# One step of a hybrid decoder on one core: LayerNorm's sums at set places between the projection's products, one-part sums of squares, factors spread without diagonals, norm vector loaded first

## The chip, the core and the metric

The kernel runs on one core of a Trainium2 chip. The metric is device time in microseconds (us), as the median of several executions. A profile is a record of one further execution, whose own time is given beside its span.

The engines named below: TensorE (PE, and PEld for its weight loads), VectorE (DVE), ScalarE (ACT), GpSimd (POOL), and SyncE (SP), which issues the transfers. Each works through its own list of instructions in order; semaphores make one wait for another.

## The reference

One layer is computed for 288 tokens (256 of a prompt, 32 of eight samples). What matters here:

```python
def layernorm(x, g, b):
    xf = x.astype(jnp.float32)
    mu = jnp.mean(xf, axis=-1, keepdims=True)
    var = jnp.mean(jnp.square(xf - mu), axis=-1, keepdims=True)
    y = (xf - mu) * lax.rsqrt(var + EPS)
    return (y * g.astype(jnp.float32) + b.astype(jnp.float32)).astype(x.dtype)
...
    h = rmsnorm(x, norm1_g)
    proj = jnp.einsum("btd,de->bte", h, w_in) + b_in
    a, gate, z = proj[..., :D_CONV], proj[..., D_CONV:2 * D_CONV], proj[..., 2 * D_CONV:]
    u = a * jax.nn.sigmoid(gate)
    u_ext = jnp.concatenate([hist_conv.astype(u.dtype), u], axis=1)
    c = jax.nn.silu(layernorm(depthwise_causal_conv(u_ext, conv_w, conv_b), ln_g, ln_b))
    z_ext = jnp.concatenate([hist_pool.astype(z.dtype), z], axis=1)
    d = multiscale_pool(z_ext, pos0)
    p = jnp.einsum("btgc,gce->btge", d, pool_w).reshape(bsz, T, D_POOL) * pool_scale
    mix = jnp.concatenate([c, p], axis=-1)
    x = x + jnp.einsum("btm,md->btd", mix, w_out)
    h2 = rmsnorm(x, norm2_g)
    f = jnp.square(jax.nn.relu(jnp.einsum("btd,df->btf", h2, w_ff1)))
    x = x + jnp.einsum("btf,fd->btd", f, w_ff2)
```

The width is 2048 (1024 of it convolution, 1024 pooling), the hidden width 8192; a last RMSNorm follows. All arrays are float32, and the states of convolution and pooling are outputs too.

## The kernel before

**Layout.** Channels lie on the 128 partitions, the 288 tokens along the free axis. `xT` holds the 16 channel tiles of x; all products give 128 output channels by 288 tokens in one PSUM bank.

**Products.** A float32 operand is split into a high part (a cast to `fp32r`, on ACT) and a low part (the rest, on VectorE or POOL). One term of a product is three matmuls: high weight by high x (L293), high weight by low x (L294), low weight by high x (L295). `gemm` does so for all k and for two banks of output channels; it takes a dictionary `between`, which calls a function ahead of a given k and holds the products from that k on behind the matmul that the function returns. Weights come 128 x 1024 at a time (`load`), are cast (L253, `whi`) and split (L258 on VectorE, L261 on POOL, `wlo`). Five buffers of `whi` and five of `wlo` are there, so a cast can wait until TensorE is done with an older block.

**Stages.** First come the input products: pairs for the eight convolution tiles (c0 to c7 of the list SEQUENCE) and for the four pooling groups, with the pooling matrices' products (L460) between them. The convolution itself is 30 multiply-adds for each tile on VectorE (L411). Then the output projection runs in two halves of eight groups with 48 products each: `project_pool` multiplies the pooling half of w_out with `mixp` and adds to `xT` (L505, the drain of a group), and the loop at L540 multiplies the convolution half with `mixc`, the normalised columns. Then the second norm, the MLP in four chunks, and the last norm with its output multiplications (L617).

**LayerNorm.** POOL adds up the convolution's tiles in `sum_c` (L420). Two matmuls with `ones` sum over the partitions (L512, `pmean`), VectorE subtracts the mean (L515), ACT squares (L517), VectorE adds three of the four squares (L521). `rsqrt_rows` makes 1/sqrt of the sums for each token and spreads it over all partitions. Then each pair of tiles is multiplied with it (L526), put through SiLU with gain and offset (L529), cast (L531) and split (L532).

**The sums of squares.** `rsqrt_sums` takes a list of parts (128 x 288 each). For each third of the tokens (96) it multiplies every part, as stationary operand, with a column of `ones` (L220), so that the tokens' sums come to lie on 96 partitions in three columns. Six small instructions form 1/sqrt (L223 to L230), then three make diagonal matrices from them (L233, `dg`), and `spread` multiplies `ones` with the diagonals (L239), which puts each factor on all partitions. It is used four times: for the first norm (`first_sums`, `first_rows`), LayerNorm, the second norm, and the last one. A float32 matmul of the program shows as two passes in the profile.

**Order.** The program is written in the order of the source, but a scheduler orders each engine's list: it takes what its own estimate of time says is ready, by a priority that follows the source. `later()` lowers the priority of the convolution's taps, and `tc.issue_after(x)` puts the instructions made within it behind x on their engine. `project_pool` before had no such places, so LayerNorm's small matmuls went between its products wherever the scheduler saw them ready. Tiles of a pool with one buffer (`ms`, which holds `pmean` and `pt`) follow each other: the next one waits until the last reader of the one before is through.

## Time and profile before

| what | us |
|---|---|
| median of 3 executions (1105.16 to 1105.8) | 1105.24 |
| the profiled execution's own time | 1111.87 |
| its span | 1110.1 |
| TensorE busy in it | 1089.5 |
| VectorE busy | 640.2 |
| ACT busy | 470.8 |

Busy times of one execution don't add up to the span, since engines work beside each other. Of the 8112 products of 128 x 288, nearly all stand back to back. In a row of the timeline the first two numbers are the start and the length of a group in us; then come the engine, the line, the operation, what it writes and reads with the tile's shape, and in brackets how long the engine had been idle before it and what ended that. Products overlap in the engine's pipeline: one of 0.29 us is followed by the next after about 0.13 us. Rows of windows give the stretch, its length, busy time and count for PE, PEld, DVE, ACT and POOL, then the granted TensorE clock, the share of the DMA engines and GB/s.

### The profile page before, as it was taken

The page shows a single profiled execution, that of the slowest core. Times are in us where ns is not written, and L with a number is a line of the kernel's source. Part 1 is how long each engine was busy: PE and PEld are TensorE (multiplying, and loading weights), DVE is VectorE, ACT ScalarE, POOL GpSimd, SP SyncE. Part 2 cuts the span into 40 slices and gives each one's busy share as a digit, 9 for nine tenths or more (in the row PEclk, how much of TensorE's full clock was granted, in tenths as well). Part 3 has the DMA queues.
Part 4 walks back from the last instruction along what each step waited for, and adds up shares of the span by engine and source line. Part 5 has one row for each costly group of instructions (what it writes and reads, how often), then busy time and mean ns, then how long its engine had stood idle before and what let it go on. Part 6 is the DMA issues. An engine that isn't in the chain of part 4 may idle for free.

```text
span 1110.1 us, 19698 instructions
## 1 busy us (share of the span) xinstructions
PE 1089.5 (98%) x8196; PEld 1086.4 (98%) x8196; DVE 640.2 (58%) x827; ACT 470.8 (42%) x577; POOL 181.5 (16%) x208
## 2 busy tenths in 40 slices
PE   9999999989999999999999999999999999999995
PEld 9999999989999999999999999999999999999995
DVE  7899999578555544445544444455544445554453
ACT  8534554466444433334443333444433334444441
POOL 0889989503000000000000000000000000000000
PEclk9999999999999999999999999999999999999998
DMA  9754467535455555555555555555555555555522
GB/s 328 246 184 147 156 179 230 180 115 171 153 170 169 160 166 170 169 163 164 170 168 162 165 171 167 163 165 171 169 160 166 172 166 163 166 171 164 164 72 86
DMA packets 57113, 187.04 MB, mean 168 GB/s; under 512 B 6080, under 2 KB 11200, under 8 KB 57024
## 3 DMA queue, kind: packets, MB, share of 16 engines
q1 hardware_dynamic: 56608, 185.52, 52.1%
q8 instruction: 64, 1.05, 0.4%
q10 hardware_dynamic: 416, 0.27, 0.1%
q14 instruction: 25, 0.20, 0.0%
HBM read 181.49 MB, written 4.28 MB: 167 GB/s over the span
## 4 chain that ended last, share of the span: by engine, by line
PE 90%; DVE 6%; POOL 2%; issue 1%; ACT 0%; DMA 0%; DVEq 0%; ACTq 0%; POOLq 0%
PE ac L293 30%; PE ac L295 30%; PE ac L294 29%; DVE pc L411 3%; POOL s L440 1%; DVE wlo L258 1%; POOL wlo L261 1%; DVE xT L617 0%; PE pt L220 0%; DMA vec<-in_vec 0%; DVE dx L452 0%; POOL prd L415 0%; DVE dx L464 0%; DVE c L417 0%; PE pt L239 0%
## 5 line engine op out<-in xcount | busy, mean ns | idle before, releaser
L253 ACT CAST whi<-wr 128x1024 fp32r<-128x1024 f32 (+1 forms) x341 | 355.6, 1043 | 569.8 <-PE ac L294 530.5
L258 DVE TENSOR_TENSOR wlo<-wr,whi 128x1024 fp32r<-128x1024 f32 (+1 forms) x300 | 371.9, 1240 | 352.3 <-ACT whi L253 351.5
L293 PE MATMUL ac<-ax,whi 128*128 128x288 f32 x1024 | 303.4, 296 | 0.0
L293 PE MATMUL ac<-fx,whi 128*128 128x288 f32 x1024 | 303.1, 296 | 0.0
L295 PE MATMUL ac<-ax,wlo 128*128 128x288 f32 x1024 | 301.9, 295 | 0.0
L295 PE MATMUL ac<-fx,wlo 128*128 128x288 f32 x1024 | 301.9, 295 | 0.0
L294 PE MATMUL ac<-ax,whi 128*128 128x288 f32 x1024 | 298.5, 292 | 0.0
L294 PE MATMUL ac<-fx,whi 128*128 128x288 f32 x1024 | 298.5, 292 | 0.0
L294 PEld LDWEIGHTS ac<-ax,whi 128*128 128x128 f32 x1024 | 192.5, 188 | 0.1
L294 PEld LDWEIGHTS ac<-fx,whi 128*128 128x128 f32 x1024 | 192.5, 188 | 0.0
L293 PEld LDWEIGHTS ac<-ax,whi 128*128 128x128 f32 x1024 | 192.4, 188 | 0.1
L293 PEld LDWEIGHTS ac<-fx,whi 128*128 128x128 f32 x1024 | 192.4, 188 | 0.0
L295 PEld LDWEIGHTS ac<-ax,wlo 128*128 128x128 f32 x1024 | 191.5, 187 | 0.0
L295 PEld LDWEIGHTS ac<-fx,wlo 128*128 128x128 f32 x1024 | 191.5, 187 | 0.0
L261 POOL TENSOR_TENSOR wlo<-wr,whi 128x512 fp32r<-128x512 f32 x82 | 108.7, 1350 | 35.3 <-ACT whi L253 35.3
L293 PE MATMUL ac<-hx,whi 128*128 128x288 f32 x384 | 113.7, 299 | 0.6 <-ACT hx L317 0.6
L294 PE MATMUL ac<-hx,whi 128*128 128x288 f32 x384 | 112.8, 296 | 0.0
L295 PE MATMUL ac<-hx,wlo 128*128 128x288 f32 x384 | 110.8, 295 | 0.0
L411 DVE SCALAR_TENSOR_TENSOR pc<-u_all,vec,pc 128x256 f32<-128x256 f32 x232 | 98.6, 479 | 0.9
L293 PEld LDWEIGHTS ac<-hx,whi 128*128 128x128 f32 x384 | 72.8, 191 | 1.0 <-ACT hx L317 0.9
L294 PEld LDWEIGHTS ac<-hx,whi 128*128 128x128 f32 x384 | 72.9, 190 | 0.1
L295 PEld LDWEIGHTS ac<-hx,wlo 128*128 128x128 f32 x384 | 72.0, 190 | 0.2 <-DVE wlo L258 0.2
(111 smaller groups left out, 811.4 us busy)
## 6 DMA issues: line engine op xcount, KB each, us to landing
wr<-in_w SPq DMA_DIRECT2D x335, 512.0 KB, 3.6
xT<-in_xT SPq DMA_DIRECT2D x7, 288.0 KB, 8.1
wr<-in_w SPq DMA_DIRECT2D x5, 256.0 KB, 3.6
out_u_out<-u_all SPq DMA_DIRECT2D x1, 1208.0 KB, 10.1
out_yT<-xT SPq DMA_DIRECT2D x2, 576.0 KB, 2.9
u_all<-in_hist_c SPq DMA_DIRECT2D x8, 136.0 KB, 5.3
out_z_out<-z_all SPq DMA_DIRECT2D x1, 668.0 KB, 8.2
z_all<-in_hist_p SPq DMA_DIRECT2D x4, 152.0 KB, 7.2
```

The source lines that it names most:

```text
L253: nc.scalar.copy(hi, raw)
L258: nc.vector.tensor_tensor(lo, raw, f32(hi), op=ALU.subtract)
L261: nc.gpsimd.tensor_tensor(lo[:, j : j + 2, :], raw[:, j : j + 2, :], f32(hi[:, j : j + 2, :]), op=ALU.subtract)
L293: nc.tensor.matmul(b, wh, xh, start=k == 0, stop=False)
L294: nc.tensor.matmul(b, wh, xl, start=False, stop=False)
L295: last = nc.tensor.matmul(b, wl, xh, start=False, stop=k == n - 1)
L411: nc.vector.scalar_tensor_tensor(out=dst, in0=up[:, w : w + SEQ], scalar=cwv[:, w : w + 1], in1=pc, op0=ALU.mult, op1=ALU.add)
L440: nc.gpsimd.tensor_tensor(s2[:, m, 2 * w - 1 :], s[:, m, 2 * w - 1 :], s[:, m, w - 1 : ZL - w], op=ALU.add)
```

## The change

- The norm vector `vec[:, 0:16]` is loaded by SyncE ahead of all else, not by ACT behind the first weights.
- `rsqrt_sums` goes over the parts first and the thirds of the tokens inside, so that all sums of one part stand together; it can put idle matmuls (`ones` by `ones`) behind the sums of each part, and makes no diagonals. `spread` multiplies each column of factors, broadcast along 128 columns as the stationary operand, with the 96 x 96 identity: three matmuls of 96 columns for one of 288.
- The first norm's spread moves from ahead of k = 1 to ahead of k = 2 of the third tile's products.
- `project_pool` and the LayerNorm code are replaced by one loop over the eight groups. The mean's two matmuls stand in group 5 ahead of k = 2, the sums in group 6 ahead of k = 3, the spread in group 7 ahead of k = 1, and from group 5 on each group stands behind the one before it. VectorE, not POOL, adds the last pair of tiles to `sum_c`, adds the fourth square too, and folds the two halves, so that one part is summed for four.
- For the second norm POOL adds the last square as well: one part for two. The last norm keeps two parts, with 3 and 6 idle matmuls behind them.

```diff
-    nc.scalar.dma_start(vec[:, 0:NG], io["vec"][:, 0:NG])
+    nc.sync.dma_start(vec[:, 0:NG], io["vec"][:, 0:NG])
...
-        for j in range(3):
-            for n, t in enumerate(parts):
-                last = nc.tensor.matmul(pt[:TB, j : j + 1], t[:, j * TB : (j + 1) * TB], ones[:, 0:1], start=n == 0, stop=n == len(parts) - 1)
+        idle = cvp.tile([P, 512], F32, name=nm("idle"), tag="cv") if sum(busy) else None
+        for n, t in enumerate(parts):
+            for j in range(3):
+                last = nc.tensor.matmul(pt[:TB, j : j + 1], t[:, j * TB : (j + 1) * TB], ones[:, 0:1], start=n + j == 0, stop=n == len(parts) - 1 and j == 2)
+            with tc.issue_after(last.ins):
+                for j in range(busy[n] if n < 2 else 0):
+                    nc.tensor.matmul(idle[:, 0:P], ones, ones, start=True, stop=True)
...
-            nc.vector.tensor_scalar(dg[:TB, j * TB : (j + 1) * TB], ident, s[2][:, j : j + 1], float(DC), op0=ALU.mult, op1=ALU.mult)
-        return dg, pq[:, 1, :T], last
...
+            last = nc.tensor.matmul(pr[:, j * TB : (j + 1) * TB], s[:, j : j + 1].to_broadcast([TB, P]), ident, start=j == 0, stop=j == 2)
+        return pr, last
...
-            if i % 2 and i > 1:
+            if i % 2 and 1 < i < N8 - 1:
...
-        third = conv_products(2, between={1: first_rows})
+        third = conv_products(2, between={2: first_rows})
...
+    def ln_mean():
+        nc.vector.tensor_tensor(sum_c, sum_c, cs[-1], op=ALU.add)
+        norm["mean"] = ms("pmean")[:, 0, :T]
+        for m in range(2):
+            last = nc.tensor.matmul(norm["mean"], ones, sum_c[:, m, :], start=m == 0, stop=m == 1)
+        return last
+
+    def ln_sums():
+        ssc = None
+        for c in cs:
+            nc.vector.tensor_tensor(c, c, norm["mean"][:, None, :].to_broadcast([P, 2, T]), op=ALU.subtract)
+            q = tmpp.tile([P, 2, T], F32, name=nm("q2"), tag="ag" if ssc is None else "ag2", bufs=2)
+            nc.scalar.activation(q, c, AF.Square)
+            if ssc is None:
+                ssc = q
+            else:
+                nc.vector.tensor_tensor(ssc, ssc, q, op=ALU.add)
+        nc.vector.tensor_tensor(ssc[:, 0, :], ssc[:, 0, :], ssc[:, 1, :], op=ALU.add)
+        norm["sums"] = rsqrt_sums([ssc[:, 0, :]], 1.0 / DC, AF.Silu)
+        return norm["sums"][2]
+
+    def ln_rows():
+        norm["rows"], last = spread(norm["sums"])
+        return last
+
+    BETWEEN = {5: {2: ln_mean}, 6: {3: ln_sums}, 7: {1: ln_rows}}
+    behind = nullcontext()
+    for g in range(8):
+        bk = bank2()
+        with behind:
+            last = gemm(each(bk), [mixp[k] for k in korder], between=BETWEEN.get(g, {}))
+        behind = tc.issue_after(last) if g > 3 else nullcontext()
+        x2 = xT[:, 2 * g : 2 * g + 2, :]
+        nc.vector.tensor_tensor(x2, x2, bk[:, :, :T], op=ALU.add)
...
-                if k < KT - 1:
-                    nc.gpsimd.tensor_tensor(ss2, ss2, q2, op=ALU.add)
+                nc.gpsimd.tensor_tensor(ss2, ss2, q2, op=ALU.add)
...
-                nc.scalar.copy(r2, rsqrt_rows([ss2, q2], 1.0 / D))
+                nc.scalar.copy(r2, rsqrt_rows([ss2], 1.0 / D))
...
-    rf = rsqrt_rows([ssf, qf], 1.0 / D)
+    rf = rsqrt_rows([ssf, qf], 1.0 / D, None, (3, 6))
```

Where the change's rows carry other line numbers: L222 are the sums (L220 before), L225 the idle matmuls, L242 the spread (L239), L228 to L235 the small chain (L223 to L230), L257 and L262 the weights' cast and split (L253, L258), L507 and L510 the mean, L516, L518 and L522 subtraction, squares and their sum, L523 the fold, L539 the drain of a pooling group (L505), L544 to L550 the normalised columns (L526 to L532). The numbers behind a name tell tiles of one name apart.

VectorE around LayerNorm's sums, before (xT with ac_2745 is the drain of group 6, L223 the first step behind the sums):

```order
L258 TENSOR_TENSOR wlo_2863<-wr_2858,whi_2862 128x1024
L521 TENSOR_TENSOR q_2486<-q_2486,q_2489 128x576
L258 TENSOR_TENSOR wlo_2867<-wr_2860,whi_2866 128x1024
L521 TENSOR_TENSOR q_2486<-q_2486,q_2493 128x576
L505 TENSOR_TENSOR xT<-xT,ac_2745 128x576
L258 TENSOR_TENSOR wlo_2926<-wr_2921,whi_2925 128x1024
L223 TENSOR_SCALAR st_2512<-pt_2499 96x3
```

and with the change (ac_2606 is group 5):

```order
L522 TENSOR_TENSOR q_2694<-q_2694,q_2697 128x576
L522 TENSOR_TENSOR q_2694<-q_2694,q_2701 128x576
L539 TENSOR_TENSOR xT<-xT,ac_2606 128x576
L522 TENSOR_TENSOR q_2694<-q_2694,q_2705 128x576
L262 TENSOR_TENSOR wlo_2823<-wr_2818,whi_2822 128x1024
L523 TENSOR_TENSOR q_2694<-q_2694 128x288
L228 TENSOR_SCALAR st_2713<-pt_2709 96x3
```

The sums moved ahead of the drain of group 6, behind the drain of group 5, the third add, one weight split and the fold.

VectorE around the first normalised columns, with the change (ac_2674 and ac_2766 are groups 6 and 7):

```order
L539 TENSOR_TENSOR xT<-xT,ac_2674 128x576
L262 TENSOR_TENSOR wlo_2914<-wr_2909,whi_2913 128x1024
L544 TENSOR_TENSOR n_2831<-c_631,pt_2709 128x576
L544 TENSOR_TENSOR n_2838<-c_721,pt_2709 128x576
L262 TENSOR_TENSOR wlo_2918<-wr_2911,whi_2917 128x1024
L539 TENSOR_TENSOR xT<-xT,ac_2766 128x576
L550 TENSOR_TENSOR mx_2835<-n_2831,mx_2835 128x2x288
```

ACT at the same place:

```order
L257 CAST whi_2913<-wr_2909 128x1024
L547 ACTIVATE n_2831<-n_2831,vec 128x288 x2
L257 CAST whi_2917<-wr_2911 128x1024
L547 ACTIVATE n_2838<-n_2838,vec 128x288 x2
L549 CAST mx_2835<-n_2831 128x2x288
L549 CAST mx_2842<-n_2838 128x2x288
```

and VectorE before (ac_2809 is group 7):

```order
L258 TENSOR_TENSOR wlo_2930<-wr_2923,whi_2929 128x1024
L505 TENSOR_TENSOR xT<-xT,ac_2809 128x576
L526 TENSOR_TENSOR n_2525<-c_633,pt_2499 128x576
L526 TENSOR_TENSOR n_2532<-c_723,pt_2499 128x576
L258 TENSOR_TENSOR wlo_2997<-wr_2992,whi_2996 128x1024
L532 TENSOR_TENSOR mx_2529<-n_2525,mx_2529 128x2x288
```

The first two multiplications moved from behind the drain of group 7 to ahead of it; the low halves (L550) still stand behind it, and a weight cast now stands between ACT's SiLUs.

TensorE's list at the end of the program, before and with the change:

```order
L220 MATMUL pt_11534<-ones,q_11531 96x1
L220 MATMUL pt_11534<-ones,ssf_3467 96x1
L220 MATMUL pt_11534<-ones,q_11531 96x1
L239 MATMUL pt_11534<-dg_11548,ones 128x288
L663 UNCONDITIONAL_BRANCH
```

```order
L299 MATMUL ac_11412<-fx_10493,wlo_11398 128x288
L222 MATMUL pt_11518<-ones,ssf_3456 96x1 x3
L225 MATMUL idle_11519<-ones 128x128 x3
L222 MATMUL pt_11518<-ones,q_11515 96x1 x3
L225 MATMUL idle_11519<-ones 128x128 x6
L242 MATMUL pt_11518<-ident,st_11535 128x96 x3
```

The three sums of the last square now stand together behind those of the rest, idle matmuls fill the two stretches behind them, and the spread reads the factors themselves.

More of the change, by code (lines that the diff above doesn't have):

```diff
@@ L497, in trunk_kernel @@
         nc.sync.dma_start(io["z_out"], z_all[:, :, ZO - PH : ZL])
-    def project_pool(groups):
-        for g in groups:
-            bk = bank2()
-            gemm(each(bk), [mixp[k] for k in korder])
-            x2 = xT[:, 2 * g : 2 * g + 2, :]
-            nc.vector.tensor_tensor(x2, x2, bk[:, :, :T], op=ALU.add)
-    project_pool(range(3))
-    pmean = ms("pmean")[:, 0, :]
-    for m in range(2):
-        nc.tensor.matmul(pmean[:, :T], ones, sum_c[:, m, :], start=m == 0, stop=m == 1)
-    ssc = None
@@ L514, in trunk_kernel @@
-    for c in cs:
-        nc.vector.tensor_tensor(c, c, both(pmean), op=ALU.subtract)
-        q = tmpp.tile([P, 2, T], F32, name=nm("q2"), tag="ag" if ssc is None else "ag2", bufs=2)
-        nc.scalar.activation(q, c, AF.Square)
-        if ssc is None:
-            ssc = q
-        elif c is not cs[-1]:
-            nc.vector.tensor_tensor(ssc, ssc, q, op=ALU.add)
-    rl = rsqrt_rows([x[:, m, :] for x in (ssc, q) for m in range(2)], 1.0 / DC, AF.Silu)
+    norm = {}
+    def ln_mean():
[4 more added lines that the diff above has]
+        return last
@@ L525, in trunk_kernel @@
         n = tmpp.tile([P, 2, T], F32, name=nm("n"), tag="ag", bufs=2)
-        nc.vector.tensor_tensor(n, c, both(rl), op=ALU.mult)
+        nc.vector.tensor_tensor(n, c, norm["rows"][:, None, :].to_broadcast([P, 2, T]), op=ALU.mult)
         for m in range(2):
@@ L533, in trunk_kernel @@
         mixc += halves((mh, ml))
-    project_pool(range(3, 8))
     x1 = []
```

9 lines of the change are left out of this document (4 added, 5 removed).

## The prediction

> **What bounds the kernel now.** I read the engines' shares first, then what TensorE waited for, then the timeline where it waited.
>
> ```profile
> PE 1089.5 (98%) x8196; PEld 1086.4 (98%) x8196; DVE 640.2 (58%) x827; ACT 470.8 (42%) x577; POOL 181.5 (16%) x208
> ...
> PE ac L293 <- ACT mx L531: 3.8, 1, 3.8
> PE pt L239 <- DVE dg L233: 2.9, 2, 1.9
> ...
> PE ac L295 <- POOL wlo L261: 0.6, 1, 0.6
> PE pp L293 <- DVE dx L464: 0.5, 1, 0.5
> ```
>
> TensorE is busy 98% of the span, so the change can only win what its products leave: a few waits, the small matmuls that stand between the products, and places where it runs at a lower clock. The second kind of view, windows with the granted clock (the number behind the busy times), shows that last part:
>
> ```profile
> 202.43:232.40 29.97, 25.91 (x189) 25.11 (x188) 18.39 (x29) 16.59 (x24) 6.31 (x6) 0.95 0.45 152
> 228.18:232.40 4.22, 3.96 (x17) 3.72 (x18) 2.73 (x4) 2.57 (x5) 0.00 (x0) 0.61 0.36 121
> ...
> 1095.00:1099.00 4.00, 1.27 (x14) 1.10 (x12) 1.81 (x9) 1.18 (x3) 0.00 (x0) 1.00 0.00 0
> 1099.00:1101.00 2.00, 1.00 (x2) 0.30 (x2) 0.91 (x3) 0.00 (x0) 0.00 (x0) 0.63 0.00 0
> ```
>
> After the 3.8 us wait the clock was 0.61 for 4.22 us, and it fell to 0.63 again at the very end. I call the eight groups of 48 products of the pool half of the output projection p0 to p7, those of the conv half c0 to c7.
>
> **The LayerNorm place, the large term.** Rows of the timeline, before:
>
> ```profile
> 196.08 0.75 DVE L505 TENSOR_TENSOR xT<-xT,ac 128x576 f32<-128x576 f32 x1 [0.47 <-PE ac L295]
> ...
> 202.43 0.76 DVE L505 TENSOR_TENSOR xT<-xT,ac 128x576 f32<-128x576 f32 x1 [2.57 <-PE ac L295]
> ...
> 210.61 0.75 DVE L505 TENSOR_TENSOR xT<-xT,ac 128x576 f32<-128x576 f32 x1
> 211.28 1.22 DVE L258 TENSOR_TENSOR wlo<-wr,whi 128x1024 fp32r<-128x1024 f32 x1
> 212.41 0.75 DVE L521 TENSOR_TENSOR q<-q,q 128x576 f32<-128x576 f32 x1
> ...
> 215.22 0.29 PE L295 MATMUL ac<-dx,wlo 128*128 128x288 f32 x1
> ...
> 215.41 1.05 ACT L253 CAST whi<-wr 128x1024 fp32r<-128x1024 f32 x1 [1.47 <-PE ac L294]
> ...
> 215.54 0.76 DVE L505 TENSOR_TENSOR xT<-xT,ac 128x576 f32<-128x576 f32 x1 [0.25 <-PE ac L295]
> ...
> 217.97 2.12 PE L220 MATMUL pt<-ones,q 128*96 128x1 f32 x24
> 219.95 0.38 PE L295 MATMUL ac<-dx,wlo 128*128 128x288 f32 x1
> ...
> 225.38 2.18 ACT L529 ACTIVATE n<-n,vec 128x288 f32<-128x288 f32 x4 [0.54 <-DVE n L526]
> 227.47 1.23 ACT L531 CAST mx<-n 128x576 fp32r<-128x576 f32 x2
> 228.16 1.43 DVE L532 TENSOR_TENSOR mx<-n,mx 128x576 fp32r<-128x576 f32 x2 [1.01 <-ACT mx L531]
> 228.18 0.53 PE L293 MATMUL ac<-mx,whi 128*128 128x288 f32 x2 [3.80 <-ACT mx L531]
> 228.97 0.51 PE L294 MATMUL ac<-mx,whi 128*128 128x288 f32 x1 [0.27 <-DVE mx L532]
> ```
>
> The drains (L505) of p3 and p4 start 6.35 us apart: 0.132 us a product. From p4's drain at 202.43 to 232.40 TensorE did p5, p6, p7 and 16 products of c0 (the seventeenth row of the window starts at its edge): 160 x 0.132 = 21.1 us, half of pmean (0.5), the 24 passes of L220 (217.97 to 219.95, so 0.082 each, 2.0) and the spread (0.5). That is 24.1 of 29.97: **5.9 us** went into waiting for the first normalised columns and into the half pace behind it. Also 12 sums become 3: 18 passes less, 18 x 0.082 = **1.5 us**.
>
> The change puts the mean into p5 behind 12 products, the sums into p6 behind 18, the spread into p7 behind 6, so that 42 products (5.5 us) cover what stood bare. A fixed place has a price, though: a product there that waits holds all products behind it. So I follow each chain by hand, with these durations.
>
> *Mean in p5.* VectorE waited 2.57 us before 202.43, so its last tap ended at 199.86. The new add (0.75) ends at 200.6; the place comes about 1.3 us after p4's drain, 203.7. Slack 3 us, no wait. What covered POOL's two adds of this sum is gone with them.
>
> *Sums in p6.* From p5's drain, VectorE has the drain (0.67 to the next, 210.61 to 211.28), the last square's add (0.67), a weight split (1.13, 211.28 to 212.41) and the half-width add (0.4, an estimate from 0.75 at full width), with the semaphore about 2.95 us. The weight split can't start sooner either: its cast waits for p5's end, as the one at 215.41. TensorE's place comes 0.32 before the drain (215.22 to 215.54), plus 0.13, plus 18 products: 2.2 us after it. **A new wait of 0.8 us**, with the rest of p6 queued behind.
>
> *Rows in p7.* From p6's drain: cast of the next weights to 0.9, its split to 2.05, two multiplications by 0.67, of which ACT takes the first at 2.8; two SiLUs (1.1), a weight cast (1.05), two SiLUs (1.1) and the cast mx (0.65) end at 6.7. c0's first product comes at 0.13 - 0.32 + 6.34 + 0.5 = 6.65. So its high half is in time, but the low half stands behind p7's own drain on VectorE: 6.84 + 0.67 + 0.8 (228.16 to 228.97) = 8.3, wanted at 6.9. **A new wait of 1.4 us.**
>
> The three narrow spreads take 6 passes, at least 0.5 us against 0.25: +0.25. Sum: -5.9 - 1.5 + 0.8 + 1.4 + 0.25 = **-4.95 us**; bounds: the waits at nothing (-7.2), and both at 2.5 us with the low clock's 2 us behind the second (-0.2).
>
> By the Trainium skill, "TensorE: Matmul & The Clock Gate" (Part 1: The HAM clock gate, the "warmup" mystery), half rate returns after an idle window of about 3.4 us; the trace agrees with its 3.8 us wait at 0.61. By that rule a wait of 1.4 us costs no clock, which is also my sum. The same page of the Trainium skill (LDWEIGHTS, loading the stationary operand) prices a weight load by its 128 columns at 1.2 GHz, 0.107 us: the three spreads would then add 0.4 instead of 0.25, and the sum would be -4.8.
>
> **First row factors.** Before, the spread waited for the diagonals:
>
> ```profile
> 35.10 0.16 DVE L230 SCALAR_TENSOR_TENSOR st<-st 96x3 f32<-96x3 f32 x1
> 35.37 0.62 DVE L233 TENSOR_SCALAR dg<-ident,st 96x96 f32<-96x96 f32 x3
> ...
> 36.05 0.75 PE L239 MATMUL pt<-dg,ones 96*128 96x288 f32 x2 [0.95 <-DVE dg L233]
> ```
>
> TensorE came at 35.10. It now comes 6 products (0.79) later, at 35.9, and the factors are there at 35.27 without the diagonals' 0.62: the 0.95 goes, 0.25 comes for the passes. But up to 172 us TensorE meets VectorE and POOL again (waits of 0.6 and 0.5 above), and these gain less than 0.95. I take **-0.5**; bounds -1.2 and +0.7, since the scheduler's order of taps and splits moves there too.
>
> **The norm vector first.**
>
> ```profile
> 0.72 0.87 SPq L181 DMA_DIRECT2D xT<-in_xT  x2
> ...
> 5.28 0.96 ACT L317 ACTIVATE hx<-xT,vec 128x288 fp32r<-128x288 f32 x2 [0.26 <-DMA vec<-in_vec]
> ...
> 7.59 0.96 ACT L317 ACTIVATE hx<-xT,vec 128x288 fp32r<-128x288 f32 x2 [0.63 <-DMA xT<-in_xT]
> ```
>
> At most 0.26 is won at the first product; SyncE's issue takes about 0.43 (two in 0.87), by which every x and weight load behind it comes later, and the next columns are waited for already (0.63). **0**, bounds -0.25 and +0.45.
>
> **Second norm.** Six passes fewer (0.5), the narrow spread +0.25: **-0.25**, bounds -0.5 and 0. POOL's fifteenth add lies far ahead of the sums:
>
> ```profile
> 283.14 1.01 POOL L569 TENSOR_TENSOR ss<-ss,q 128x288 f32<-128x288 f32 x1 [4.35 <-ACT q L567]
> ...
> 300.40 0.65 PE L239 MATMUL pt<-dg,ones 96*128 96x288 f32 x2
> ...
> 300.67 0.51 PE L293 MATMUL ac<-ax,whi 128*128 128x288 f32 x1
> ...
> 301.08 0.40 ACT L580 COPY r<-pt 128x288 f32<-128x288 f32 x1 [1.90 <-PE pt L239]
> ```
>
> The next product starts 0.27 us behind the wide spread at full clock, and its reader 0.68 us.
>
> **The end.** Nothing covers this stretch:
>
> ```profile
> 1.03 4.21 PE L203 MATMUL warm<-ones 128*128 128x128 f32 x18 [1.03 <-DVE ones L193]
> ...
> 1096.19 0.33 PE L220 MATMUL pt<-ones,q 128*96 128x1 f32 x2 [0.93 <-ACT q L605]
> ...
> 1096.89 0.31 PE L220 MATMUL pt<-ones,q 128*96 128x1 f32 x2
> ...
> 1098.45 0.62 DVE L233 TENSOR_SCALAR dg<-ident,st 96x96 f32<-96x96 f32 x3
> ...
> 1099.13 1.00 PE L239 MATMUL pt<-dg,ones 96*128 96x288 f32 x2 [1.93 <-DVE dg L233]
> 1100.17 5.28 DVE L617 TENSOR_TENSOR xT<-xT,pt 128x288 f32<-128x288 f32 x6 [1.09 <-PE pt L239]
> ```
>
> Behind the last square stood five pairs of passes, 0.175 apart; now three: -0.35. The diagonals go, 1098.45 to 1099.13: -0.65. The spread took 1.04 to its reader at clock 0.63; at full clock 0.68 plus 0.25 for the passes: -0.1. The filling matmuls are to hold that clock: 18 passes of the same kind took 4.21 us at the start, 0.23 each, so about 0.115 at full clock (an estimate); 6 of them end near 1096.2, when the square arrives, 12 near 1098.1, when the factors do. **-1.1**, bounds -1.4 and -0.5 (fillings late).
>
> **Sum:** 0 - 0.5 - 4.95 - 0.25 - 1.1 = -6.8 us. The profiled execution's 1111.87 (span 1110.1) would be 1105.1; from the median of 1105.24 it is **1098.4 us**.
>
> **Rivals.**
> - *The second wait falls cold or grows.* At c0 the low half lands later than I count, or the short waits in p6 and at c0 add up for the clock: 228.18 to 232.40 shows about 2 us lost at 0.61, and another us of wait. For: three engines meet there, in program order. Against: from 1095 to 1099 TensorE was busy for 1.27 of 4 us and its clock stayed at 1.00. -6.8 + 3 = -3.8: 1101.4.
> - *The gain at LayerNorm doesn't come.* ACT's weight cast between the SiLUs waits for a buffer that only p7's end frees, and c0 stands bare as before. For: in this kernel casts do wait on TensorE (215.41). Against: five buffers, and by their order this cast needs p7's first half alone. Then -1.5 is left of the passes, +0.8 for the sums, +0.25, and -1.85 elsewhere: -2.3, with the lower bounds elsewhere about -1, 1104.2.
> - *Slower: the mean's fixed place meets late taps.* VectorE and POOL set the pace up to 172 us, and a wait put badly into that new order, as the two of 0.6 and 0.5 above, delays all taps behind it. Each us beyond the 3 us of slack in p5 is a us on TensorE. It decides from 3 + 6.8, about 10 us of delay; at 12 us, for instance, the time is 1105.24 - 6.8 + 9 = 1107.4. Against: VectorE stood idle 2.57 us before 202.43.
>
> **How the numbers follow.** Forecast 0.62, cold or longer wait 0.22, no gain at LayerNorm 0.08, slower 0.08. 0.2% (2.2 us) is about what a measurement here can tell from none: faster is below 1103.0, which the first two give: 0.84; the third is same, 0.08; the fourth slower, 0.08. The forecast's own range is 1096 to 1100.5 from its bounds; down to 1095 the range holds the waits at nothing with the better bounds of the end and the start, up to 1103 the second case.
>
> **What would show it.** In the changed profile: no wait of TensorE for mx above 2 us and no window near 0.61 at c0; a wait of about 0.8 for the sums in p6 (L222) and 1.4 for mx's low half; no wait at the first spread; factors to the first output multiplication without L233 in between, clock 1.00 up to it. Wrong I would be if TensorE waits at the mean (L510), if waits in the taps' stage grow by more than a us, or if the last spread takes over a us.

## The result, and the profile after

| | us |
|---|---|
| changed kernel, median of 20 executions (1106.72 to 1110.62) | 1109.04 |
| kernel before, median of 20 executions beside it (1104.4 to 1117.46) | 1108.16 |
| ratio, with its 95% interval | 0.9993 [0.9973, 1.0012] |
| profiled execution after: its time, span | 1109.48, 1107.7 |
| forecast | 1098.4, range 1095 to 1103 |

No difference could be measured, where 6.8 us less had been forecast. The median of the kernel before says little, since its executions form two groups: over all comparisons of this study 93 of 153 lie below 1109 (median 1106.05) and 60 above (median 1112.4), with nothing between 1109.0 and 1111.1. The changed kernel has one group, with its median between the two. The three executions of the forecast's starting time (1105.24) were of the lower group, the profiled one (1111.87) of the upper.

First the two profiles, stage by stage, from the start times of the same instructions:

| stage | before | after | change | forecast |
|---|---|---|---|---|
| to the first norm's sums | 32.04 | 32.77 | +0.73 | 0 |
| on to the drain of p4 | 170.39 | 170.37 | -0.02 | -0.5 |
| on to the last drain of the conv half (LayerNorm) | 78.88 | 77.51 | -1.37 | -4.95 |
| on to the last group's drain (second norm, MLP) | 813.90 | 813.58 | -0.32 | -0.25 |
| on to the first output multiplication | 4.96 | 3.87 | -1.09 | -1.1 |
| to the end | 9.89 | 9.57 | -0.32 | 0 |
| span | 1110.06 | 1107.67 | -2.39 | -6.8 |

Half of pmean (0.5 us) ran ahead of p4's drain before and stands behind it now, so at equal work the LayerNorm's stage changed by -1.9 and the one ahead of it by +0.5. The second and the last norm came out as forecast. The last row goes with the vector's load: it is 9.56 to 9.57 us in the eight profiles of this study that load the vector first, and 9.88 to 9.91 in the twelve others; why is not shown. Rows of the timeline of the changed kernel at the second norm's spread and at the end:

```profile
299.10 0.80 PE L242 MATMUL pt<-ident,st 96*128 96x96 f32 x6
299.94 0.40 ACT L595 COPY r<-pt 128x288 f32<-128x288 f32 x1 [1.93 <-PE pt L242]
...
1094.48 0.91 PE L225 MATMUL idle<-ones 128*128 128x128 f32 x6
1095.23 0.65 PE L222 MATMUL pt<-ones,q 128*96 128x1 f32 x6
1095.74 1.58 PE L225 MATMUL idle<-ones 128*128 128x128 f32 x12
...
1097.16 0.90 PE L242 MATMUL pt<-ident,st 96*128 96x96 f32 x6
1098.10 3.65 DVE L632 TENSOR_TENSOR xT<-xT,pt 128x288 f32<-128x288 f32 x4 [1.00 <-PE pt L242]
```

The narrow spread takes 0.84 us to its reader (299.10 to 299.94) against 0.68 for the wide one. At the end the 12 fillings last 1.58 us and reach up to the spread, which starts at 1097.16.

What TensorE waited for after the change, longest in total first (total, times, longest):

```profile
PE pt L222 <- DVE q L523: 2.3, 1, 2.3
PE ac L297 <- DVE xT L539: 1.4, 2, 0.7
PE ac L297 <- ACT whi L257: 1.4, 1, 1.4
PE ac L299 <- POOL wlo L265: 1.2, 1, 1.2
```

The 3.8 us in front of c0 are gone, and so are the waits for the diagonals. The first row is new, and it is where the LayerNorm's gain stayed. Its timeline:

```profile
208.41 3.06 POOL L265 TENSOR_TENSOR wlo<-wr,whi 128x512 fp32r<-128x512 f32 x2 [1.75 <-ACT whi L257]
208.95 3.14 DVE L522 TENSOR_TENSOR q<-q,q 128x576 f32<-128x576 f32 x2 [0.50 <-ACT q L518]
...
212.01 0.74 DVE L539 TENSOR_TENSOR xT<-xT,ac 128x576 f32<-128x576 f32 x1
...
215.07 0.64 PE L222 MATMUL pt<-ones,q 128*96 128x1 f32 x6 [2.27 <-DVE q L523]
...
228.17 0.29 PE L297 MATMUL ac<-mx,whi 128*128 128x288 f32 x1
229.18 0.40 PE L297 MATMUL ac<-mx,whi 128*128 128x288 f32 x1 [0.72 <-DVE xT L539]
229.85 0.40 PE L298 MATMUL ac<-mx,whi 128*128 128x288 f32 x1 [0.27 <-DVE mx L550]
230.09 0.30 PE L299 MATMUL ac<-mx,wlo 128*128 128x288 f32 x1
```

Two adds of squares took 3.14 us, 1.57 each where 0.75 had been counted, while POOL split p7's weights beside them. So p5's drain came at 212.01, the add of the last square behind it, and the sums in p6 stood 2.27 us. At c0 the first four products start at 228.17, 229.18, 229.85 and 230.09, where full pace is 0.13 apart: 1.92 - 0.40 = 1.5 us lost to p7's drain and the low half behind it, close to the 1.4 forecast. The clock stayed at 1.00.

Windows of the changed kernel (start:end, length, busy PE, PEld, DVE, ACT, POOL with counts, clock, DMA share, GB/s):

```profile
10.00:12.00 2.00, 1.69 (x11) 1.46 (x11) 1.91 (x3) 2.00 (x5) 0.00 (x0) 1.00 1.05 407
12.00:16.00 4.00, 4.00 (x21) 4.00 (x20) 4.00 (x7) 4.00 (x8) 0.00 (x0) 0.57 1.04 392
...
216.00:217.00 1.00, 1.00 (x9) 1.00 (x8) 0.65 (x4) 0.98 (x2) 0.00 (x0) 0.94 0.84 266
217.00:218.00 1.00, 1.00 (x6) 1.00 (x5) 0.00 (x0) 0.99 (x3) 0.00 (x0) 0.50 0.46 180
218.00:219.00 1.00, 1.00 (x6) 1.00 (x6) 0.37 (x1) 0.59 (x1) 0.00 (x0) 0.50 0.00 0
219.00:220.00 1.00, 1.00 (x6) 1.00 (x6) 0.85 (x1) 0.00 (x0) 0.00 (x0) 0.50 0.00 0
220.00:221.00 1.00, 1.00 (x8) 1.00 (x8) 0.00 (x0) 0.00 (x0) 0.00 (x0) 0.85 0.33 41
...
500.00:700.00 200.00, 200.00 (x1514) 200.00 (x1514) 94.51 (x86) 75.06 (x77) 0.00 (x0) 1.00 0.51 166
```

Behind the 2.27 us wait the clock was at half for 0.12 + 3 + 0.30 = 3.4 us (0.94 and 0.85 are mixtures of 1.0 and 0.5), which costs 1.7 us of work. The same happened at 12 to 16 us. The last row shows the pace of the MLP's products, 1514 in 200 us; it becomes the main matter below.

### The profile page after: what moved, and what is told of

Read it like the earlier page. It is cut to its first block, busy times and chain, and to the rows that moved or that the text cites. A ratio compares the mean times of both kernels' runs of the same rounds, so it can differ in the third digit from the quotient of the medians.

```text
span 1107.7 us, 19709 instructions
## 1 busy us (share of the span) xinstructions
PE 1090.3 (98%) x8206; PEld 1088.1 (98%) x8206; DVE 637.8 (58%) x818; ACT 470.1 (42%) x577; POOL 181.6 (16%) x207
## 4 chain that ended last, share of the span: by engine, by line
PE 93%; DVE 4%; ACT 1%; POOL 1%; issue 0%; DMA 0%; SPq 0%; DVEq 0%; POOLq 0%; ACTq 0%
PE ac L297 31%; PE ac L299 31%; PE ac L298 30%; DVE pc L415 2%; POOL wlo L265 1%; DVE wlo L262 1%; DVE xT L632 0%; DMA wr<-in_w 0%; DVE q L522 0%; ACT whi L257 0%; PE pt L242 0%; PE pt L222 0%; DVE c L421 0%; PE idle L225 0%; DVE dx L468 0%
## 5 line engine op out<-in xcount | busy, mean ns | idle before, releaser
L257 ACT CAST whi<-wr 128x1024 fp32r<-128x1024 f32 (+1 forms) x341 | 355.4, 1043 | 568.0 <-PE ac L298 534.6
L262 DVE TENSOR_TENSOR wlo<-wr,whi 128x1024 fp32r<-128x1024 f32 (+1 forms) x300 | 368.9, 1230 | 359.1 <-ACT whi L257 358.2
```

The lines of the kernel that those rows point to most:

```text
L257: nc.scalar.copy(hi, raw)
L262: nc.vector.tensor_tensor(lo, raw, f32(hi), op=ALU.subtract)
```

## The experiments

Medians are given with the number of executions. Since the kernel before is in two groups, kernels are compared with each other, and with the group they share a pace with.

**The kernel before, unchanged**, to see its groups (e0; the runs are named by their labels).

> The kernel before, unchanged, timed as an own kernel, to see how far its own executions lie apart. Its 20 times beside the changed kernel were not one heap: ten from 1104.4 to 1107.4, nine from 1112.0 to 1117.5. Theory A (the change saves 1.4 us at LayerNorm, 0.3 at the second norm and 1.1 at the end, and gives 0.7 back at the start): the 2.4 us between the profiled executions are the effect, and the kernel before is 0.2% slower than the changed kernel when both are taken in the same session. Theory B (the starting time of 1105.24 was simply a low draw): the times here again fall on both sides of 1109, with a ratio to the kernel before of 1.000 and an interval of some tenths of a per cent.

1106.67 (12 executions, 1105.23 to 1116.25), seven below 1107 and five above 1111; the profile was of the upper group (1112.03). Theory B holds: the two groups are the kernel's own. In these executions, and in those of the kernel before beside them, the mean granted clock is 0.991 to 0.994 in both groups, so the clock isn't what separates them.

**e1: the norm vector's load back on ACT's queue**, rest as changed.

```diff
-    nc.sync.dma_start(vec[:, 0:NG], io["vec"][:, 0:NG])
+    nc.scalar.dma_start(vec[:, 0:NG], io["vec"][:, 0:NG])
```

> The changed kernel with the norm vector's load back on ACT's queue. Theory (SyncE's loads behind it came later, and an earlier first product only ran dry): first product back near 5.9 us, no dry wait of 1.4 us near 10 us, the sums of the first norm (L222) near 32.0 instead of 32.8, time 0.7 us below the changed kernel. Rival (the start is bound by the transfers' total, saturated up to 22 us, wherever the vector stands in the queue): the sums come at 32.8 again, time the same to 0.2 us.

1107.74 (12), 1.3 below the changed kernel. The sums came at 31.87, but one step of the theory fell: the wait near 10 us was there all the same. Two rows of this kernel's timeline:

```profile
5.83 0.66 PE L297 MATMUL ac<-hx,whi 128*128 128x288 f32 x3 [1.02 <-ACT hx L321]
10.75 0.40 PE L297 MATMUL ac<-hx,whi 128*128 128x288 f32 x1 [1.29 <-ACT whi L257]
```

What it lacks is the half clock behind the wait. Over all profiles of this study, six of the eight with the vector first had a half clock of 3.4 us near 12 to 16 us, and one of the twelve with the vector on ACT's queue (in two others, the profile before and e10, the products ran at half pace up to about 10 us). The first norm's sums came at 32.77 to 33.66 us in the six, at 31.63 (e4) and 32.08 (e15) in the two that load the vector first and kept the clock, and at 31.53 to 32.04 with the vector on ACT's queue, but at 33.50 in the one of these that lost the clock (e17). So moving the load costs through the clock, in most executions and not in all.

**e2 and e3: LayerNorm's sums 18 products later in p6**, alone, and with the vector back on ACT's queue.

```diff
-    BETWEEN = {5: {2: ln_mean}, 6: {3: ln_sums}, 7: {1: ln_rows}}
+    BETWEEN = {5: {2: ln_mean}, 6: {6: ln_sums}, 7: {1: ln_rows}}
```

> The changed kernel with the LayerNorm's sums 18 products later in p6 (behind 36 products instead of 18). Theory (what ate the LayerNorm's gain is the 2.27 us wait for the last square's sum and the half pace behind it): these 18 products last 2.37 us, so the wait at L222 falls to under 0.3, the granted clock stays above 0.9 in the 10 us behind it, and the span falls by about 3.8 us (2.27 + 1.6) less what the later factors cost at c0, where the wait of 0.7 may grow; time 2 to 4 us below the changed kernel. Rival (the wait only moves to c0, because the multiplications, SiLUs and splits behind the factors set the time): L222 doesn't wait, but the waits for mx in front of c0 grow by as much as is won, time the same to 0.5 us.

> Both edits: the norm vector's load on ACT's queue and the sums 18 products later in p6. Theory: the two gains are in different stages and add: 0.7 at the start and 2 to 4 at LayerNorm, together 3 to 5 us below the changed kernel. Rival (the start only shifts the phase of what follows): the sum of both differs from the two alone by more than 1 us.

1104.65 (9) and 1103.89 (6): 4.4 and 5.15 below the changed kernel, each a little more than the upper end of what was expected. The sums' row in the first of them has no wait any more:

```profile
215.65 0.64 PE L222 MATMUL pt<-ones,q 128*96 128x1 f32 x6
```

The clock stays at 1.00 behind it, the waits in front of c0 didn't grow, and from p4's drain to the last drain of the conv half it takes 73.54 us instead of 77.51. The rival falls: the wait didn't move to c0.

**e4: POOL's split beside the adds left out**: p7's second half of weights gets no lower part, its products take the upper part twice.

```diff
-WAYS = {"c2": "GVGV", "c": "GGGV", "p": "GVVG", "w": "GG", "ff": "VV"}
+WAYS = {"c2": "GVGV", "c": "GGGV", "p": "GVVG", "w": "GG", "w7": "GN", "ff": "VV"}
...
+            if way == "N":
+                nc.scalar.copy(parts[-1][0], raw)
+                parts[-1][1] = parts[-1][0]
```

> The changed kernel without the split that POOL does beside the squares' adds in p5: for the second half of p7's weights no lower part is computed, the products take the upper part in its place (same count and shapes). Theory (the adds take 1.57 us each instead of 0.75 because POOL works beside them, and that delays p5's drain and the square's last sum): the two adds of L522 in p5 take about 1.5 to 1.7 us instead of 3.14, p5's drain comes 1.4 us sooner, the wait at the sums (L222) falls from 2.27 to about 0.8, as the prediction had it; time 1.4 us below the changed kernel, and 1.7 more if the half pace behind the wait goes too. Rival (ACT's squares and casts set the pace there): the wait stays above 1.8, time the same to 0.5 us.

1105.22 (10), 3.8 below the changed kernel. Its timeline:

```profile
207.67 1.62 DVE L527 TENSOR_TENSOR q<-q,q 128x576 f32<-128x576 f32 x2 [0.50 <-ACT q L523]
...
212.27 0.64 PE L222 MATMUL pt<-ones,q 128*96 128x1 f32 x6 [0.75 <-DVE q L528]
```

The two adds take 1.62 instead of 3.14, and TensorE waits 0.75 for the sums: the 0.8 of the prediction. Behind this wait the clock stayed at 1.00, and from p4's drain to the last drain of the conv half it takes 74.40 us instead of 77.51: POOL's split cost 1.5 us by the wait and 1.7 by the clock. (The profile also lacks the half clock at the start, with the first norm's sums at 31.63 instead of 32.77; not every execution need lack it.)

**e5: fillings in the wait**: 18 passes ahead of the sums in p6.

```diff
+        fill = cvp.tile([P, 512], F32, name=nm("fill"), tag="cv")
+        for j in range(9):
+            nc.tensor.matmul(fill[:, 0:P], ones, ones, start=True, stop=True)
         norm["sums"] = rsqrt_sums([ssc[:, 0, :]], 1.0 / DC, AF.Silu)
```

> The changed kernel with 18 passes of ones by ones into an unused bank ahead of the LayerNorm's sums in p6, in the 2.27 us wait (12 such passes took 1.58 at the end, so 18 take about 2.4). Theory (this wait costs twice: its own length and the half clock of 3.4 us behind it): the sums come at the same 215.1, the clock behind them stays at 1.0, time 1.7 us below the changed kernel (half of 3.4 us). Rival (the half clock has another cause, the thin work of p5 to p7 or a fixed period): the clock falls to 0.5 all the same behind the sums, time the same to 0.3 us or 0.1 to 0.3 longer.

1107.11 (10), 1.9 below the changed kernel (1.6 of it between p4's drain and the last drain of the conv half), though TensorE does more and the square's last sum comes no sooner. Rows of the timeline and of the windows:

```profile
213.00 2.17 PE L526 MATMUL fill<-ones 128*128 128x128 f32 x18
215.43 0.64 PE L222 MATMUL pt<-ones,q 128*96 128x1 f32 x6 [0.26 <-DVE q L523]
```

```profile
217.00:218.00 1.00, 1.00 (x10) 1.00 (x9) 0.26 (x2) 0.99 (x3) 0.00 (x0) 1.00 0.86 311
218.00:219.00 1.00, 1.00 (x10) 1.00 (x9) 0.00 (x1) 0.96 (x2) 0.00 (x0) 1.00 0.09 33
```

Ten instructions in a us where the changed kernel had six. The half clock was the second price of the wait.

**e6: LayerNorm as before**, everything else as changed (`project_pool` and `pmean` at their old places, four squares into 24 passes, the sum of all tiles on POOL).

> The changed kernel with the LayerNorm as before (mean, sums and factors at their old places, four squares summed by 24 passes) and everything else as changed: start, narrow spreads, second norm, end. Theory A (the changed LayerNorm is worth about 1.4 to 1.9 us against the profiled kernel before): 1110.5 to 1111.5 us, one heap; the 3.8 us wait for mx is back, with a half clock behind it. Theory B (the two heaps of the kernel before, 1106 and 1112.5, come from the bare wait in front of c0): the times here again fall in two heaps about 6 us apart, near 1104.5 and 1110.5. Rival to B (the heaps come from the start, with the norm vector on ACT's queue): one heap.

1110.9 (12, 1109.45 to 1112.13), 1.9 above the changed kernel, in one group. The wait is back:

```profile
PE ac L297 <- ACT mx L535: 3.6, 1, 3.6
```

So the changed LayerNorm is worth 1.9 us, and theory B falls: with this wait back there is still one group.

**e7, e10 and e11: the kernel before three times more**, to get a profile of the lower group.

> The kernel before once more, for a second profile: if this execution falls in the lower heap near 1106, its trace shows what the 6 us are. Theory (the wait in front of c0 and the half clock behind it are shorter or gone): the stage from p4's drain to the second norm is some 5 us shorter, the stages ahead and behind are the same. Rival (the gap is in the start or the taps): the drain of p4 comes 5 us sooner, the rest is the same.

> The kernel before once more, to get a profile of an execution near 1106. Expected: about an even chance for either heap; in a lower one the missing 6 us lie in one stage, in front of c0 by the theory that the bare wait is shorter there, or in every product (0.8 ns of 132) by its rival.

> The same again, with the same expectation as the run ahead of it.

1111.79, 1111.5 and 1106.32. The third is of the lower group, and its waits are those of the others: 3.8 for mx, 2.9 for the diagonals. The last drain of the conv half is at 282.45, even later than in the profiles of the upper group (280.68 to 281.73). What differs is the pace of the MLP. One window of the lower execution, and the same of the upper one from which the prediction was made:

```profile
500.00:700.00 200.00, 200.00 (x1528) 200.00 (x1527) 95.40 (x88) 76.08 (x79) 0.00 (x0) 1.00 0.54 167
```

```profile
500.00:700.00 200.00, 200.00 (x1515) 200.00 (x1514) 94.72 (x87) 75.87 (x79) 0.00 (x0) 1.00 0.52 166
```

At the same clock and with TensorE busy throughout, 1528 products against 1515. By the start times from 400 to 1000 us a product takes 131.11 ns in the lower execution, in a rhythm of 126.7, 133.3, 133.3, and 132.22 in the upper one, in a rhythm of several values from 125 to 138. From 300 us to the end of the MLP there are some 6000 products: 6000 x 1.11 ns = 6.7 us, the gap between the groups; the stage from the conv half's last drain to the last group's drain took 807.21 us here against 813.90. The theory of the bare wait falls. Its rival (every product) holds for the products behind the second norm alone: from 240 to 280 us all twenty profiles have 304 or 305 products in 40 us, which by the start times is 132.2 ns a product, the slow rhythm. So every profiled execution comes to the second norm slow, and some leave it quick.

The two rhythms stand in one more place, from the first norm's spread to the pooling matrices' first products near 116 us. The profile before and the changed one:

```profile
50.00:110.00 60.00, 60.00 (x460) 60.00 (x459) 58.14 (x124) 25.64 (x34) 52.73 (x53) 1.00 0.51 168
```

```profile
50.00:110.00 60.00, 60.00 (x456) 60.00 (x456) 57.82 (x124) 25.48 (x34) 53.19 (x52) 1.00 0.51 167
```

Here the profile before is quick (131.1 ns a product) and the changed one slow (132.2), over some 600 products: 0.7 us. Of the seven profiles with the first norm's wide spread, four are quick there (before, e10, e11, e15) and three slow (e0, e7, e8); the thirteen with the narrow one are all slow. What an execution does here doesn't tell what it does behind the second norm.

**e8: the vector's load alone** on the kernel before (the line of e1, the other way round), and **e9: all but start and LayerNorm** (e6 with the vector's load on ACT's queue).

> The kernel before with the norm vector's load moved to SyncE's queue, nothing else changed. Theory (the edit costs where it is alone too: an earlier first product runs dry, and a half clock of 3.4 us falls behind it in most executions): the first sums come 0.7 to 1.5 us later than in the kernel before, time 0.7 to 1.5 above the upper heap of before, near 1113. If the two heaps of the kernel before come from its start, there is one heap; if they come from elsewhere, two, 6 us apart.

> The kernel before with the narrow spreads, the first norm's factors one step later, the shorter sums of squares and the filled end; start and LayerNorm as before. Theory (the end is worth 1.1 us, the second norm 0.3, the first factors nothing): 1110 to 1110.5, that is 1.4 to 1.9 below the upper heap of before (1112). If the two heaps of before come from the diagonals or the unfilled end, there is one heap here; if from the bare LayerNorm with the vector on ACT's queue, two, 6 us apart.

The first: 1105.89 (11, 1104.0 to 1107.1), not the 1113 expected. By its time every execution was in the quick rhythm (the profile has 1527 products in the window), though only a load far ahead was moved, and in the profile the first sums came 1.3 us later than in the kernel before (33.38), as expected. The second: 1110.85 (11, 1109.2 to 1112.4), by its time every one in the slow rhythm (1515 in the profile), 0.4 above what was expected. So a change of the program can fix the rhythm in one state or the other, and what fixes it can be cheap in itself.

**e15: the changed second norm on top of the vector's load**, that is, on the kernel whose executions were all quick.

```diff
-                if k < KT - 1:
-                    nc.gpsimd.tensor_tensor(ss2, ss2, q2, op=ALU.add)
+                nc.gpsimd.tensor_tensor(ss2, ss2, q2, op=ALU.add)
...
-                nc.scalar.copy(r2, rsqrt_rows([ss2, q2], 1.0 / D))
+                nc.scalar.copy(r2, spread_narrow(rsqrt_sums([ss2], 1.0 / D, narrow=True)))
```

> The kernel before with the norm vector's load first (whose eleven executions were all in the quick rhythm, 1104.0 to 1107.1) and, on top, the changed second norm alone: one-part sum of 6 passes, narrow spread. Theory (the changed second norm saves 0.3 us where it stands and loses the quick rhythm): all executions near 1112.3 (1105.9 - 0.3 + 6.7), 1513 to 1515 products in 200 us of the feed-forward. Rival (the rhythm is set elsewhere): near 1105.6.

1112.8 (10, 1110.85 to 1115.92): 6.9 more than without it. Its window:

```profile
500.00:700.00 200.00, 200.00 (x1515) 200.00 (x1514) 94.76 (x87) 75.98 (x79) 0.00 (x0) 1.00 0.53 166
```

The same stage's start-to-start times in this trace, in ns, ahead of the six passes of the spread and behind them:

```
ahead:  130 126 131 134 132 131 132 131 133 130 126 131 134 132 131 132 131 133   mean 131.1
behind: 133 131 132 134 128 133 136 126 132 133 132 133 137 126 132 133 133 132   mean 132.0
```

The products ran quick between sums and spread, and slow from the spread on: the six passes of the narrow spread turned the rhythm. The profile of e6 has the same turn at this place, from 131.3 ns a product to 132.2.

**e12, e13 and e14: variants of the second norm** on the kernel of e3: as before (12 passes of two parts, diagonals, wide spread); one part and wide spread; two parts and narrow spread.

```diff
-                nc.scalar.copy(r2, rsqrt_rows([ss2], 1.0 / D))
+                nc.scalar.copy(r2, spread_wide(rsqrt_sums([ss2, q2], 1.0 / D, by_part=False)))
...
+                nc.scalar.copy(r2, spread_wide(rsqrt_sums([ss2], 1.0 / D)))
...
+                nc.scalar.copy(r2, spread(rsqrt_sums([ss2, q2], 1.0 / D, by_part=False))[0])
```

> Both edits (vector's load on ACT's queue, LayerNorm's sums 18 products later) and the second norm as before: POOL's fourteen adds, two parts summed by 12 passes, diagonals and the wide spread. Theory (the feed-forward's 6000 products run in one of two rhythms, 131.1 or 132.2 ns a product, and what TensorE does at the second norm sets which): part or all of the executions fall into the quick rhythm, near 1097.5 (1103.9 - 6.7 + 0.3), the others near 1104.2; windows behind 300 us show 1526 products in 200 us in the quick ones and 1513 to 1515 in the others. Rival (the rhythm comes from the LayerNorm's or the start's form): all near 1104.

> Both edits, and at the second norm only the wide spread from diagonals back, with the one-part sum of 6 passes kept. Theory with the spread as the cause: some executions near 1097, the others near 1104. Theory with the sums' passes as the cause (behind the 12 passes of the quick execution the products already ran in another rhythm, ahead of the spread): all near 1104, 1513 to 1515 products in 200 us.

> Both edits, and at the second norm only the two-part sums of 12 passes back, with the narrow spread kept. Theory with the sums' passes as the cause: some or all executions near 1097.5. Theory with the spread as the cause: all near 1104.5.

1104.23 (10), 1104.24 (10) and 1098.03 (4, 1097.53 to 1098.21). The quick executions that were expected of part of e12 didn't come. The third kernel is quick:

```profile
500.00:700.00 200.00, 200.00 (x1528) 200.00 (x1527) 95.72 (x88) 77.27 (x80) 0.00 (x0) 1.00 0.54 168
```

Neither the spread nor the passes decide alone: 12 passes with the wide spread are slow in e12, mixed in the kernel before, and always quick in e8. In e14 the products ran slow up to the narrow spread (132.4) and quick behind it (131.1): the same six passes that turn quick to slow in e15. It hangs on how the stream of products meets the break.

**e16: the changed kernel with 12 passes at the second norm** (the third variant's line), nothing else undone, and **e17: the kernel of e14 again**.

> The changed kernel with one thing undone: the two-part sums of 12 passes at the second norm (the narrow spread stays). Theory (the changed second norm took the quick rhythm from this kernel, and 12 passes ahead of the narrow spread give it back): 1102.5 to 1103.5 (1109.0 - 6.7 + 0.5), 1526 to 1528 products in 200 us. Rival (the rhythm also depends on how the stages ahead end, so that 12 passes help only with the other two edits): some or all executions near 1109.5.

> The kernel of the run with both edits and 12 passes once more, in more rounds: vector's load on ACT's queue, LayerNorm's sums 18 products later, 12 passes at the second norm. Theory (its four executions near 1098 were no accident): all executions between 1097 and 1100, a ratio to the kernel before near 0.991 over both of its heaps. Rival (this kernel has two heaps as well): some near 1104.

1103.66 (11, 1100.61 to 1106.04), 5.4 below the changed kernel, with 1528 products in the same window. So in the changed kernel the two-part sum at the second norm (and with it one add less on POOL) is enough to bring the quick rhythm:

```profile
500.00:700.00 200.00, 200.00 (x1528) 200.00 (x1527) 95.26 (x88) 76.59 (x79) 0.00 (x0) 1.00 0.54 168
```

The best version repeats: 1097.97 (6, 1097.36 to 1099.53), a ratio to the kernel before of 0.9914 [0.9887, 0.9941]. It is 8.1 us below the lower group of the kernel before (1106.05).

## Why the prediction was wrong

**The starting point, and the second norm's -0.25.** The sum was made against a profiled execution of 1111.87 and then taken from a median of 1105.24, as if the 6.6 us between them were nothing but a shift. They are a property of the product stream that the change touches: by their times, 60% of the executions of the kernel before run the MLP at 131.1 ns a product, and none of the changed kernel's twenty does. The step "Six passes fewer (0.5), the narrow spread +0.25: -0.25" was right for what stands at the second norm (-0.32) and missed what the edit does to the 6000 products behind it: +6.7 us for every execution that had been quick, shown by e15 (+6.9 on a kernel that was always quick) and e16 (-5.4 when undone). It isn't the second norm's form by itself: with the old form e8 was always quick and e12, behind the changed first norm and LayerNorm, never. Against the upper group's median, whose pace it shares, the changed kernel is 1112.4 - 1109.0 = 3.4 us faster. So of the 10.6 us between 1098.4 and 1109.0 the pace is 6.35 (1112.4 against 1106.05) and the terms of the sum, 3.4 instead of 6.8, are 3.4; the other 0.8 is that 1105.24, from three executions, lay below the median of its own group.

**LayerNorm, -4.95, came as -1.4 to -1.9** (profiles; e6). The 5.9 us at c0 went as said, the mean in p5 waited for nothing, and c0 lost 1.5 us and no clock, where 1.4 was said. The step that failed is "a new wait of 0.8 us" for the sums. From p5's drain to the sums the chain took 3.06 us (212.01 to 215.07), as counted (2.95). But it was counted from a drain that VectorE takes up as soon as TensorE is through with p5, and here VectorE still had two adds of squares, which took 1.57 each beside POOL's split, where adds beside an idle POOL (at 212.41 before) take 0.75. The wait was 2.27 (+1.5), and with it came a half clock of 3.4 us (+1.7): 3.2 of the 3.6 us that are missing; the half of pmean that moved into this stage (0.5) is about the rest. Leave POOL's split out, and the wait is 0.75 (e4); fill the wait, and the clock stays (e5); move the sums out of reach, and both go (e2, -4.4).

By the Trainium skill, "SBUF — State Buffer" (Who interferes with whom), a VectorE instruction with both inputs in SBUF contends with a GpSimd one that reads there, and the one that comes second is blocked until the first is through. The trace agrees: 3.14 against 1.62 us for two adds. The prediction didn't look for it.

**The clock.** Forecast was that a wait of 1.4 us costs none, which held at c0; for the sums, the waits were thought too short to matter. By the Trainium skill, "TensorE: Matmul & The Clock Gate" (Part 1: The HAM clock gate, the "warmup" mystery), activity is watched in a free-running window of about 3.4 us. The trace agrees with the length, in blocks of 3.4 us at half; but the prediction had read it as an idle time of 3.4 us that must pass, and 2.27 us were enough here (as in e1 and e16, with waits of 2.27 and 2.28), while 0.75 (e4) was not.

**Start, 0, came as +0.73**, beyond its bound of +0.45 that counted SyncE's issues alone. What cost was again a half clock, at 12 to 16 us, in six of eight profiles with the vector first. **First factors, -0.5, came as 0**: at their own place they won 1.1 us, more than was said (the 0.95 wait went, and products that stood 0.74 later than before ahead of the spread stood 0.38 earlier behind it). Behind it 0.7 was lost to the slow rhythm up to the pooling products, a cost that the prediction had in no term; that the new spread, narrow and six products later, keeps it slow there is likely from the twenty profiles (13 of 13 slow, 3 of 7 with the old one) but was not tested alone. Of the waits, POOL's split grew from 0.6 to 1.2, one of 0.7 for a drain is new (at 183.79), and one of 0.5 at 172.44 is gone; such waits the prediction had named. Half of pmean (0.5) left the stretch.

**The end, -1.1, came as -1.09**, by the steps named: three pairs of passes instead of five, no diagonals, clock at 1.00 up to the spread.

**The rivals.** "The second wait falls cold or grows" had the right mechanism at the wrong of its two places: the sums in p6, not c0. "The gain at LayerNorm doesn't come" (c0 as bare as before) didn't occur: the 3.8 us in front of c0 went. Nor did the slower rival (late taps at the mean): there was no wait at the mean, so that its 1107.4 lies nearest to the result is chance. That an edit would change the pace of the products behind it was in none of them, and none of the three signs of being wrong was seen: no wait at the mean, no growth of the taps' waits by more than a us, and a last spread of 0.90 us.

## What to carry over

Look at the spread of the executions before taking a median as the base: two groups are a mechanism, and a profile belongs to one of them. Compare the count of products in a long stretch without waits between profiles; a difference of 1% there outweighs most edits of small matmuls, and should be tested by varying the few instructions that break the stream. When a chain is moved beside other work, take each duration from a place with the same neighbours, above all VectorE's adds beside POOL, and price a wait on TensorE like the 2.27 us here with the half clock behind it (1.7 us); filling passes kept the clock (e5).

## What the runs showed of the hardware

- A stream of products (128x288, a weight load for each) keeps one of two rhythms for 800 us, 131.1 or 132.2 ns a product at full clock. A break of a few small matmuls (6 or 12 passes of one column, or the spread) sets which. What in the break decides stays open: at the second norm, 6 passes with the narrow spread were slow in all of e1 to e6, e9, e15 and the changed kernel, and 6 with the wide spread in e13; 12 with the narrow spread were quick in e14, e16 and e17; 12 with the wide spread were quick in e8, slow in e12, and either in the kernel before.
- Half clock inside the kernel comes in blocks of 3.4 us, or two of them (e0, e6 and e15 behind the wait in front of c0). How a wait ends in it differs between executions of one kernel: behind the same 3.80 us the kernel before had two blocks in e0 and one in the profile before, e7, e10 and e11; near 11 us a wait of 1.49 brought none in e14 and one of 1.41 a block in e17, the same kernel.
- Two VectorE adds of 128x576 took 3.14 us beside two POOL splits of 128x512 (3.06 together) and 1.62 without them (e4).
